# A one-core decoder layer in split float32: more loads on SyncE's queue, squares summed by ScalarE, and low parts of 22 weight pieces made by accumulating transfers

## The chip, the cores and the metric

The kernel runs on one core of a Trainium2 chip. The core has five engines with programs of their own: TensorE (PE, matmuls and transposes), VectorE (DVE), ScalarE (ACT), GpSimd (POOL) and SyncE (SP, here an issuer of transfers only). The metric is the device time of one launch in microseconds; the median of three runs is compared. The time before is 680.02 us (679.84 to 684.64).

## The reference, cut to what matters

One layer of a decoder trunk for 512 tokens of width 1024, all in float32:

```python
h = rmsnorm(x, norm_mix); mem_h = rmsnorm(mem, norm_mem)
proj = h @ w_in                                  # one input projection, cut into 8 parts
c_q, c_kv, k_rope, hq, hf, hi, hg, mq = split(proj)
y_mla = mla_group(c_q, c_kv, k_rope, ...)        # low-rank attention, causal, 4 heads
y_hg  = hgrn2_group(hq, hf, hi, hg, ...)         # gated linear recurrence, 4 heads
y_mem = mem_group(mq, mem_h, ...)                # cross-attention into 256 memory tokens
x = x + concat([rmsnorm(y_mla), y_hg, rmsnorm(y_mem)]) @ w_out
x = x + (silu(h2 @ w_gate) * (h2 @ w_up)) @ w_down      # h2 = rmsnorm(x), inner width 2816
```

`rmsnorm(x, g)` is `x * rsqrt(mean(x*x) + eps) * g`.

## The kernel before, in words

Activations are kept transposed, with features on the 128 partitions and the 512 tokens along the row; x is eight tiles of 128 x 512 (`xin`, tag "tm"). To keep float32 accuracy on PE, every operand is split into a high part, rounded to PE's float32r format, and a low part, the rest; `mm3` (L558) makes a product of three matmuls: high by high, high by low, low by high. `split` (L528) makes the parts: the high part is a cast on ACT, the low part a subtraction on DVE. The gain of the first norm is multiplied in while x is split; the factor 1/rms of each token is applied later, to products: `rx` (per token as a column) and `RX` (the same, spread over a 128 x 512 tile).

The program runs in this order. Twelve matmuls on constants come first (`WARM`, L437). Then x is loaded with the first columns of `w_in` (the `we` tiles, four feature blocks at once), split, and multiplied into four accumulators. `gated` makes the q and f parts of the recurrent group, `wide` (L735) its values, four 128-token blocks at a time, and `hg_levels` its decays. `lowrank` makes the compressed q and kv. The attention of the first group, the memory's keys and values, the cross-attention and the output projection follow, and from about 340 us on the FFN, in three column groups with seven products each for blocks of two by two (`seven`, L1410). There the sum of two weight blocks is already made by transfers which add to what lies in the destination: GpSimd issues them (`more`, L1424, `accum_op=ALU.add`).

Weights arrive by `load` (L536): 512 KB at a time into one of three 128 x 1024 tiles "wr", issued by SP. `piece` splits half a tile into a pair of 128 x 512 tiles, "wh" (five slots) and "wl" (four slots). In the FFN `part` also uses "wr" tiles for pairs.

Sums of squares: for x, ACT squares each of the eight tiles, DVE adds them up (`sumsq`), PE sums the result over the partitions with matmuls of 32 columns by 2 (`colsums`, `T.tiles`), and DVE makes the reciprocal root by some ten small steps (`rms`, `rsqrt_col`). For the memory the same is done with four tiles. 

What sets the order: nothing is issued while the program is recorded. `Recorder.record` lists every operation with its inputs and a priority (its number and a class, changed by the table `NUDGE`: from, to, shift), and `Recorder.run` then lays them out on five engines by estimated costs and free slots; some operations may be moved to another engine. `issue` emits them in that order, from L421 (PE's small tiles) and L424 (all the rest), so nearly all rows of the profile have one of these two lines, and the names of tiles tell them apart: "xh" and "xl" are the parts of x, "mx" and "v" the parts of the first weights, "at", "mm" and "tr" the accumulators' banks (three, three and two).

Of the kernel before, what the change touches and what calls it, by code (L numbers as in the profile page):

```python
# [47 lines left out]
class Recorder:  # L48
# [205 lines left out]
    def length(self, o):  # L254
# [3 lines left out]
        return 2 if o.name == "transpose" or o.kw["rhs"].dtype != F32 else 4  # L258


    IDLE = (1500, 3400)


    NUDGE = ((4523, 4572, -1208), (2899, 2922, 153), (3591, 3619, 261), (5080, 5112, 35), (5132, 5152, -187), (4881, 4888, -127), (833, 873, 7059), (4038, 4040, 343), (3730, 3774, 191), (4055, 4056, -1089), (5057, 5087, 605), (5096, 5097, 51), (5041, 5094, -195), (5387, 5394, 57), (3008, 3017, 415), (3705, 3738, -1018), (969, 989, -566), (5497, 5507, 388), (3048, 3063, 528), (4794, 4826, -14), (4034, 4058, 24), (5265, 5278, -2632), (5519, 5549, -317), (4066, 4083, -4), (968, 978, -1195), (4416, 4437, -227), (5057, 5066, -584), (3678, 3726, 79), (2213, 2230, 387), (3749, 3800, -698), (3952, 4008, -75), (290, 314, 354), (4141, 4157, 211), (586, 592, 790), (2631, 2650, 56), (3575, 3624, -28), (371, 421, 128), (5155, 5160, 312), (685, 697, 401), (2820, 2830, 265), (4487, 4528, -350), (763, 784, -147), (4472, 4519, 334), (1209, 1222, 357), (2030, 2049, -600), (3663, 3706, 33), (1550, 1566, 8), (369, 379, 609), (2292, 2334, 1893), (3104, 3108, -229), (3446, 3497, -146), (3458, 3487, 401), (5080, 5128, 17), (3070, 3075, 53), (2112, 2117, 110), (1594, 1603, -13), (1503, 1505, 92), (1400, 1404, 1034), (3047, 3065, -458), (2398, 2422, -345), (3844, 3904, -190), (3156, 3169, 94), (1128, 1180, -33), (3732, 3757, 144), (2990, 3037, -207), (3971, 3973, -124), (1839, 1844, -36), (1248, 1276, -13), (1792, 1793, -366), (158, 195, -424), (2647, 2648, 611), (5037, 5054, 66), (4876, 4882, -106), (1471, 1483, -459), (2041, 2058, -88), (2747, 2771, -122), (1486, 1489, 331), (1523, 1542, 1379), (693, 698, -494), (4462, 4511, -166), (1167, 1213, -456), (3349, 3388, 638), (1775, 1778, -455), (3988, 4008, -390), (1981, 2008, -332), (2573, 2761, -42), (1036, 1062, 17), (1336, 1355, 86), (675, 700, -238), (1554, 1556, -17), (1880, 1936, 59), (2818, 2836, -24), (3075, 3091, -674), (4376, 4379, 398), (731, 737, -425), (2690, 2706, -44), (2646, 2647, 42), (2917, 2971, -572), (4832, 4835, -140), (5153, 5162, 438), (4481, 4514, -137), (5422, 5428, 274), (3705, 3761, -89), (4234, 4235, -182), (1261, 1283, 34), (62, 109, -1000015), (1830, 1889, 12), (2099, 2105, 41), (3735, 3746, 267), (4336, 4337, 1074), (710, 740, -88), (2697, 2724, -320), (2183, 2208, -18), (2625, 2651, -21), (4345, 4401, -177), (4291, 4292, 38), (3298, 3301, -1000015), (2682, 2739, 63), (3480, 3487, -804), (629, 670, 295), (3160, 3163, -148), (506, 518, 651), (3695, 3706, -432), (59, 112, -15), (2898, 2925, 47), (5531, 5583, 85), (2275, 2320, -999980), (2355, 2360, -999779), (5131, 5139, 36), (2523, 2552, -11), (3090, 3546, -33), (1181, 1182, -4), (3436, 3446, 73), (3880, 3930, -29), (1824, 1825, -202), (543, 566, -23), (722, 758, 559), (1736, 1753, -372), (1890, 1897, -9), (2502, 2532, -5), (165, 167, 493), (5584, 5595, 398), (4277, 4283, 21), (4888, 4893, 37), (2286, 2317, 647), (3287, 3324, 419), (822, 884, -497), (2242, 2289, 81), (2797, 2822, -89), (1448, 1478, 373), (1100, 1164, 5), (2563, 2568, -8), (597, 604, 388), (3827, 3833, 55), (2186, 2188, 205), (558, 569, -25), (817, 860, 405), (2749, 2796, -79), (3691, 3740, -109), (2604, 2716, 54), (4296, 4345, -525), (3222, 3238, -12), (5421, 5451, 334), (2642, 2653, 4), (2042, 2047, 655), (4097, 4148, 5), (2643, 2666, -47), (4973, 4974, 614), (4924, 4927, 36), (552, 567, 653), (3734, 3738, -105), (726, 727, -195), (4433, 4436, 151), (4710, 4711, 303), (5121, 5134, -12), (4502, 4550, -60), (503, 512, -603), (3731, 3736, 544), (3839, 3851, -13), (1180, 1184, 101), (3659, 3694, 52), (5258, 5622, -1035), (5522, 5533, 84), (2598, 2602, 41), (2394, 2411, 45), (849, 857, -233), (2961, 2977, 85), (2625, 2657, -152), (139, 181, -39), (1176, 1182, 305), (3429, 3430, -555), (4813, 4828, 6), (893, 946, 81), (4741, 4745, 17), (3304, 3348, -251), (1057, 1079, -612), (4202, 4231, -64), (374, 405, 161), (5386, 5625, 1000335), (2718, 2754, -1000022), (2645, 2647, 4), (3911, 3957, 21), (3971, 4017, 33), (2755, 2781, 564), (5202, 5217, -999393), (2812, 2821, 17), (5518, 5557, -114), (2442, 2452, -175), (4376, 4419, 25), (4811, 4835, 8), (2472, 2500, -52), (1746, 1788, 413), (4968, 4969, 508), (1150, 1211, 451), (4566, 4588, -192), (1898, 1916, -5), (1400, 1411, 417), (3557, 3654, -8), (2519, 2521, 130), (2693, 2698, 180), (3237, 3290, 11), (3775, 3779, 268), (2140, 2143, 57), (4141, 4153, 14), (2237, 2240, 187), (3139, 3141, 177), (677, 684, 54), (1788, 1791, -237), (3385, 3418, 24), (2394, 2412, 54), (2524, 2550, -13), (1887, 1901, 19), (3423, 3485, -72), (4991, 5053, 35), (3834, 3844, -59), (1153, 1164, -8), (3326, 3345, 218), (3302, 3317, -567), (1923, 1972, 828), (4940, 4941, 63), (4555, 4581, 224), (2297, 2359, -29), (4778, 4807, -998879), (1766, 1771, -78), (2837, 2854, 7), (252, 266, 415), (246, 279, -363), (3968, 3972, -612), (5235, 5249, -10), (1534, 1544, -588), (3486, 3502, -1000043), (5217, 5226, -357), (5611, 5625, -72), (4595, 4615, -184), (4896, 4916, 266), (1756, 1791, 11), (3224, 3227, -171), (4428, 4443, -6), (2740, 2757, 171), (513, 519, -1000400), (1665, 1716, 690), (5093, 5096, -296), (3135, 3182, 17), (1773, 1789, 51), (656, 673, -363), (5199, 5203, -53), (5201, 5257, 328), (4968, 5016, -50), (1569, 1575, 376))

    def run(self):
        ops = self.ops
        for a, b, d in self.NUDGE:
            for o in ops[a:b]:
                o.prio += d  # L270
# [21 lines left out]
        while done < len(ops):  # L292
# [89 lines left out]
            for k in o.new:  # L382
                tag = self.tiles[k][0]
                slots[tag].remove(min(slots[tag]))
                order[tag].remove(k)
# [1292 lines left out]
```

## Time and profile before

| | |
|---|---|
| median of 3 runs | 680.02 us |
| profiled execution | 681.25 us |
| its span, first to last instruction | 679.5 us |
| PE busy | 672.0 us |
| DVE busy | 590.7 us |
| ACT busy | 396.1 us |
| POOL busy | 100.1 us |
| bytes moved | 95.16 MB |

The span is what the rows below divide; the profiled execution is 1.75 us longer than it. PE's busy time counts a matmul until its results have passed, so neighbouring matmuls overlap in it (a row of 0.39 us every 0.23 us), and how fast PE works is read from the starts. An accumulating transfer has its own queue in the list of queues (software_dynamic), since GpSimd issues it; SP's and ACT's are hardware_dynamic.

### The profile page before, as it was taken

The page shows a single profiled execution, that of the slowest core. Times are in us where ns is not written, and L with a number is a line of the kernel's source. Part 1 is how long each engine was busy: PE and PEld are TensorE (multiplying, and loading weights), DVE is VectorE, ACT ScalarE, POOL GpSimd, SP SyncE. Part 2 cuts the span into 40 slices and gives each one's busy share as a digit, 9 for nine tenths or more (in the row PEclk, how much of TensorE's full clock was granted, in tenths as well). Part 3 has the DMA queues.
Part 4 walks back from the last instruction along what each step waited for, and adds up shares of the span by engine and source line. Part 5 has one row for each costly group of instructions (what it writes and reads, how often), then busy time and mean ns, then how long its engine had stood idle before and what let it go on. Part 6 is the DMA issues. An engine that isn't in the chain of part 4 may idle for free.

```text
span 679.5 us, 12872 instructions
## 1 busy us (share of the span) xinstructions
PE 672.0 (99%) x4686; PEld 563.7 (83%) x4686; DVE 590.7 (87%) x1316; ACT 396.1 (58%) x779; POOL 100.1 (15%) x134
## 2 busy tenths in 40 slices
PE   9999999999999999999999999999999999999997
PEld 5889987788887888788888888888888899889986
DVE  6878889769989889887989989779898979998996
ACT  7674355547667665765577555456545554754662
POOL 1000000000000000000023222323222223323320
PEclk9999999999999999999999999999999999999999
DMA  9512320014233243134358887987977789978755
GB/s 314 169 50 68 123 75 29 32 65 139 79 125 125 77 140 110 31 110 156 109 128 155 219 197 186 172 204 172 207 166 171 160 176 215 202 163 178 161 101 143
DMA packets 48159, 95.16 MB, mean 140 GB/s; under 512 B 5472, under 2 KB 13536, under 8 KB 48096
## 3 DMA queue, kind: packets, MB, share of 16 engines
q1 hardware_dynamic: 32256, 67.33, 30.3%
q0 software_dynamic: 15120, 25.96, 24.1%
q10 hardware_dynamic: 720, 1.05, 0.5%
q8 instruction: 37, 0.61, 0.4%
q14 instruction: 26, 0.21, 0.1%
HBM read 92.22 MB, written 2.10 MB: 139 GB/s over the span
## 4 chain that ended last, share of the span: by engine, by line
PE 94%; DVE 3%; DMA 1%; ACT 1%; issue 0%; SPq 0%; DVEq 0%
PE mm L424 54%; PE at L424 32%; PE tr L424 6%; PE at L421 1%; DMA tm<-in_xT 1%; DVE sm L424 1%; PE tr L421 1%; DMA tm<-in_xn 1%; DVE y L424 0%; DVE tc L424 0%; DVE tm L424 0%; DVE hd L424 0%; DVE wl L424 0%; DVE v L424 0%; SPq L424 0%
## 5 line engine op out<-in xcount | busy, mean ns | idle before, releaser
L424 ACT CAST wr<-mx 128x512 fp32r<-128x512 f32 (+1 forms) x78 | 45.7, 595 | 40.0 <-PE at L424 25.7
L424 ACT CAST wh<-wr 128x512 fp32r<-128x512 f32 (+2 forms) x75 | 43.9, 597 | 40.7 <-PE mm L424 28.8
L424 DVE TENSOR_TENSOR wr<-mx,wr 128x512 fp32r<-128x512 f32 (+1 forms) x94 | 60.6, 655 | 6.3 <-ACT wr L424 5.0
L424 DVE TENSOR_TENSOR wl<-wr,wh 128x512 fp32r<-128x512 f32 (+2 forms) x84 | 54.9, 657 | 8.3 <-PE mm L424 6.7
L424 ACT CAST wh<-mx 128x512 fp32r<-128x512 f32 (+1 forms) x74 | 43.8, 598 | 30.3 <-PE at L424 16.2
L424 PE MATMUL mm<-xh,wh 128*128 128x512 f32 x136 | 53.8, 396 | 0.4 <-DVE hd L424 0.4
L424 PE MATMUL mm<-xl,wh 128*128 128x512 f32 x136 | 54.1, 399 | 0.0
L424 DVE TENSOR_TENSOR wl<-mx,wh 128x512 fp32r<-128x512 f32 (+1 forms) x81 | 51.9, 654 | 2.5 <-PE at L424 2.0
L424 PE MATMUL mm<-xh,wl 128*128 128x512 f32 x136 | 53.4, 394 | 0.0
L424 POOL DMA_DIRECT2D mx<-in_wg x36 | 31.6, 950 | 121.5 <-DVE wr L424 78.6
L424 PE MATMUL mm<-wh,xh 128*128 128x512 f32 (+2 forms) x136 | 47.2, 371 | 0.0
L424 ACT CAST wh<-y 128x512 fp32r<-128x512 f32 (+1 forms) x51 | 30.1, 594 | 28.2 <-PE at L424 13.7
L424 PE MATMUL mm<-wh,hd 128*128 128x512 f32 (+2 forms) x140 | 44.7, 366 | 0.3 <-DVE qr L424 0.3
L424 PE MATMUL mm<-wh,mx 128*128 128x512 f32 x128 | 43.6, 401 | 0.0
L424 POOL DMA_DIRECT2D mx<-in_wu x36 | 31.4, 936 | 81.9 <-DVE wr L424 31.9
L424 POOL DMA_DIRECT2D mx<-in_wd x33 | 28.8, 938 | 71.8 <-DVE wl L424 50.5
L424 DVE TENSOR_TENSOR wl<-y,wh 128x512 fp32r<-128x512 f32 (+1 forms) x52 | 33.2, 649 | 2.1 <-PE at L424 1.2
L424 POOL MEMSET pb<- 128x128 f32 x15 | 2.8, 205 | 214.8 <-PE at L424 203.6
L424 PE MATMUL mm<-wl,xh 128*128 128x512 f32 (+2 forms) x92 | 32.8, 359 | 0.0
L424 PE MATMUL mm<-v,xh 128*128 128x512 f32 x96 | 31.8, 401 | 0.0
L424 PE MATMUL at<-wh,xh 128*128 128x512 f32 x88 | 31.5, 391 | 0.0
L424 PEld LDWEIGHTS mm<-xh,wh 128*128 128x128 f32 x136 | 25.6, 188 | 5.8 <-DVE hd L424 0.9
(469 smaller groups left out, 1950.0 us busy)
## 6 DMA issues: line engine op xcount, KB each, us to landing
wr<-in_wf SPq DMA_DIRECT2D x17, 512.0 KB, 3.7
mx<-in_wd POOLq DMA_DIRECT2D x33, 256.0 KB, 4.6
wr<-in_wo SPq DMA_DIRECT2D x12, 512.0 KB, 3.7
mx<-in_wg POOLq DMA_DIRECT2D x24, 256.0 KB, 6.1
mx<-in_wu POOLq DMA_DIRECT2D x24, 256.0 KB, 5.8
mx<-in_wd SPq DMA_DIRECT2D x22, 256.0 KB, 4.0
y<-in_wd SPq DMA_DIRECT2D x22, 256.0 KB, 4.5
wr<-in_wt SPq DMA_DIRECT2D x8, 512.0 KB, 3.2
```

Of the source, the lines that this page charges most:

```text
L421: r = self.nc.tensor.matmul(get(a), lhsT=get(b), rhs=get(c), start=first, stop=last, skip_group_check=True)
L424: r = getattr(getattr(self.nc, o.eng), o.name)(*[get(a) for a in o.args], **{k: get(a) for k, a in o.kw.items()})
```

## The change: what it does

- The weights of x's first tiles are issued by SP for all tiles but the first (before, ACT issued those of the first four), and the number of warm-up matmuls is 9 instead of 12.
- `squares` replaces the sums of squares of x and of memory: x (and memory) is loaded once more with tokens on the partitions, ACT squares each half row and sums it in the same instruction (`accum_out`), and one DVE addition joins the halves. The additions of `sumsq` and the column sums on PE are left out for these two.
- `load` is gone. Each piece of 512 columns or fewer is its own transfer of up to 256 KB into one of six 128 x 512 "wr" tiles.
- For 22 pieces (features 0 to 4, `wva` and `wvb`, named in `MADE`) the low part is made in another way: ACT writes minus the high part into "wl", and a transfer issued by GpSimd adds the weight itself to it.
- In `softmax` the small negation moves from DVE to ACT.
- The planner is told a shorter landing time for early transfers, and `NUDGE` has 249 other entries instead of 269.

```diff
-    NUDGE = ((4523, 4572, -1208), (2899, 2922, 153), (3591, 3619, 261), ...
+    NUDGE = ((2674, 2759, 2137852), (4855, 4871, -117), (3907, 3920, 369), ...
...
-WARM = 12
+WARM = 9
 FIRST = 4
-EARLY = {k: (1, ("wr", "p", "p", "tc", "tc", "tc", "hd", "hd")[k]) for k in range(8)}
-XLAG = 0
+EARLY = {k: (1, ("qr", "p", "p", "tc", "tc", "tc", "hd", "hd")[k]) for k in range(8)}
+MADE = {0: 'S', 1: 'S', 2: 'S', 3: 'S', 4: 'S', 'wva': 'S', 'wvb': 'S'}
...
-        "wr": 3, "wh": 5, "wl": 4, "xh": 8, ...
+        "wr": 6, "wh": 5, "wl": 4, "xh": 8, ...
...
+    def piece(src, a, b, made=False, tags=("wh", "wl")):
+
+        w = slice(0, b - a)
...
+        raw = sb("wr")[:, w]
+        hi = sb(tags[0], dt=F32R)[:, w]
+        lo = sb(tags[1], dt=F32R)[:, w]
         with rec.first(0):
-            split(raw[:, a:b], hi[:, :b - a], lo[:, :b - a])
+            DMA.dma_start(out=raw, in_=src[:, a:b])
+            if made:
+                A.copy(hi, raw)
+                A.activation(lo, f(hi), AF.Copy, scale=-1.0)
+                G.dma_start(out=lo, in_=src[:, a:b], accum_op=ALU.add)
+            else:
+                split(raw, hi, lo)
         return hi, lo
...
-                    (A if k < 4 else DMA).dma_start(out=w, in_=t["we"][k - 1])
+                    DMA.dma_start(out=w, in_=t["we"][k - 1])
...
-    xs = None
-    for k in range(KD):
-        with rec.after(xdone[min(KD - 1, k + XLAG)]), rec.first(0):
-            xs = sumsq(xraw[k:k + 1], xs, "td", V)
...
+    def squares(src, nb, tag, cls):
+
+        v = small(2 * nb).rearrange("p (b j) -> p b j", j=2)
+        for b in range(nb):
+            for j in range(2):
+                r = sb(tag)
+                with rec.first(cls):
+                    DMA.dma_start(out=r, in_=src[b, j])
+                A.activation(sb("td"), r, AF.Square, accum_out=v[:, b, j:j + 1])
+        r = small(nb)
+        V.tensor_tensor(r, v[:, :, 0], v[:, :, 1], ALU.add)
+        V.tensor_scalar(r, r, RC / D, RC * EPS, ALU.mult, ALU.add)
+        return rsqrt_col(r, nb)
...
-        V.tensor_copy(rx, rms(xs, D))
+        V.tensor_copy(rx, squares(t["xn"], NB, "y", -1))
...
-            ms = sumsq([r.rearrange("p a b -> p (a b)")], ms)
-        ms2 = sb("td", (P, NM))
-        V.tensor_tensor(ms2, ms[:, :NM], ms[:, NM:], ALU.add)
         rm = cp.tile([P, 2], F32, name="rm")
-        vm = small(2)
-        V.tensor_scalar(vm, colsum(ms2, 2), RC / D, RC * EPS, ALU.mult, ALU.add)
-        V.tensor_copy(rm, rsqrt_col(vm, 2))
+        V.tensor_copy(rm, squares(t["mem"], 2, "y", 1))
...
-        V.tensor_scalar(m, m, neg, None, ALU.mult)
+        A.activation(m, m, AF.Copy, scale=neg)
```

How the order moves is shown at three places, with the line of the kernel, the operation, its output and inputs, and its size.

PE at the start, from the last warm-up matmul on ("tr" from a constant), before:

```order
L424 MATMUL tr_1797<-const-bfloat16-1.0 128x512
L424 MATMUL at_1860<-xh_1851,mx_1843 128x512
L424 MATMUL mm_1863<-xh_1851,mx_1843 128x512
L424 MATMUL at_1869<-xh_1851,mx_1843 128x512
L424 MATMUL at_1860<-xl_1858,mx_1843 128x512
L424 MATMUL at_1860<-xh_1851,v_1846 128x512
```

and in the changed kernel:

```order
L426 MATMUL tr_1962<-const-bfloat16-1.0 128x512
L426 MATMUL at_2009<-xh_2000,mx_1992 128x512
L426 MATMUL at_2009<-xl_2007,mx_1992 128x512
L426 MATMUL at_2009<-xh_2000,v_1995 128x512
L426 MATMUL at_2023<-xh_2000,mx_1992 128x512
L426 MATMUL at_2025<-xh_2000,mx_1992 128x512
```

The low part of x ("xl") is asked for by the second matmul now, by the fourth before.

GpSimd's program behind its first memsets, before (the memsets after "tm" belong to the attention):

```order
L424 MEMSET tm_1975 128x512
L424 MEMSET tm_1996 128x512
L424 MEMSET pb_3477 128x128
L424 MEMSET pb_3481 128x128
L424 MEMSET pb_3538 128x128
```

and in the changed kernel, where ten more accumulating transfers from in_wf stand behind the twelve from in_wva and in_wvb:

```order
L426 MEMSET tm_2134 128x512
L426 MEMSET tm_2144 128x512
L426 DMA wl_2425<-in_wva 128x320
L426 DMA wl_2477<-in_wva 128x320
L426 DMA wl_2501<-in_wva 128x320
L426 DMA wl_2523<-in_wva 128x320
L426 DMA wl_2563<-in_wva 128x320
```

The 22 transfers have one fixed order on GpSimd's queue, ahead of the memsets of the attention.

PE in the changed kernel where the values of the recurrent group begin ("mm_2520", "mm_2528", "tr_2537" and "tr_2544" are the accumulators of four token blocks, "wh" and "wl" the weight's parts). First the end of the group ahead and the first piece:

```order
L426 MATMUL mm_2468<-xl_2171,wh_2356 128x512
L426 MATMUL mm_2468<-xh_2166,wl_2398 128x512
L426 MATMUL mm_2520<-wh_2391,xh_2000 128x320
L426 MATMUL mm_2520<-wl_2425,xh_2000 128x320
L426 MATMUL mm_2520<-wh_2391,xl_2007 128x320
```

and, 36 rows further, the first matmul with the low part of the fourth piece:

```order
L426 MATMUL mm_2528<-wl_2501,xh_2062 128x320
L426 MATMUL mm_2528<-wh_2466,xl_2072 128x320
L426 MATMUL mm_2528<-wh_2498,xh_2088 128x320
L426 MATMUL mm_2520<-wl_2523,xh_2088 128x320
L426 MATMUL mm_2520<-wh_2498,xl_2097 128x320
L423 MATMUL at_2623<-pth_2318,tm_2482 32x32 x16
```

Between the last use of wl_2398 and the first of wl_2523 stand 40 matmuls of 320 columns.

## Rows read from the trace of the kernel before

**Rows 1.** The page's first part: busy time, share of the span and instructions of each engine.

```profile
PE 672.0 (99%) x4686; PEld 563.7 (83%) x4686; DVE 590.7 (87%) x1316; ACT 396.1 (58%) x779; POOL 100.1 (15%) x134
```

**Rows 2.** The page's slices, 40 of 17 us each: PE's granted clock in tenths, and GB/s of the transfers.

```profile
PEclk9999999999999999999999999999999999999999
...
GB/s 314 169 50 68 123 75 29 32 65 139 79 125 125 77 140 110 31 110 156 109 128 155 219 197 186 172 204 172 207 166 171 160 176 215 202 163 178 161 101 143
```

**Rows 3.** The timeline of PE in the FFN, from 440 us on: start, length in us, engine, line, operation, output and inputs.

```profile
439.94 0.39 PE L424 MATMUL mm<-wr,hd 128*128 128x512 f32 x1
440.17 0.39 PE L424 MATMUL at<-wh,hd 128*128 128x512 f32 x1
```

**Rows 4.** The page's chain of work that ended last, by engine.

```profile
PE 94%; DVE 3%; DMA 1%; ACT 1%; issue 0%; SPq 0%; DVEq 0%
```

**Rows 5.** The list of what PE waited for: tile and engine waited for, us in total, times, longest.

```profile
PE tr L421 <- issue: 0.9, 1, 0.9
PE tr L424 <- PEq L1667: 0.8, 1, 0.8
PE at L424 <- ACT xh L424: 0.6, 1, 0.6
PE mm L424 <- DVE hd L424: 0.4, 1, 0.4
PE mm L424 <- DVE qr L424: 0.3, 1, 0.3
PE at L424 <- ACT mx L424: 0.3, 1, 0.3
PE mm L424 <- DVE xl L424: 0.2, 1, 0.2
```

**Rows 6.** The timeline at the start (PE, ACT and DVE) and, in the last line, PE's last matmul. In brackets the idle time before and what ended it.

```profile
0.78 4.95 PE L424 MATMUL tr<-const-bfloat16-1.0 128*128 128x512 bf16 x12 [0.78 <-PEq L1667]
...
5.55 0.72 ACT L424 ACTIVATE xh<-tm,wr 128x512 fp32r<-128x512 f32 x1 [2.40 <-DMA wr<-in_web]
...
6.31 0.75 DVE L424 SCALAR_TENSOR_TENSOR xl<-tm,wr,xh 128x512 fp32r<-128x512 f32 x1 [1.94 <-ACT xh L424]
...
6.33 0.50 PE L424 MATMUL at<-xh,mx 128*128 128x512 f32 x1 [0.60 <-ACT xh L424]
...
6.73 0.50 PE L424 MATMUL mm<-xh,mx 128*128 128x512 f32 x1
...
7.07 0.39 PE L424 MATMUL at<-xh,mx 128*128 128x512 f32 x1
...
9.80 0.50 PE L424 MATMUL at<-xh,mx 128*128 128x512 f32 x1 [0.26 <-ACT mx L424]
...
675.24 0.39 PE L424 MATMUL mm<-wh,xh 128*128 128x512 f32 x1
```

**Rows 7.** Starts on PE around the column sum of x (the matmul ahead of it and the second one behind it, a line that merges two), and pieces of the chain of waits in order of time (start, us, what): the column sum of memory, and the matmuls behind the column sums in which PE waited longest.

```profile
21.65 0.39 PE L424 MATMUL at<-xh,mx 128*128 128x512 f32 x1
...
22.67 0.62 PE L424 MATMUL at<-xh,v 128*128 128x512 f32 x2
...
95.04 0.24 PE tr L421 x16
...
136.46 2.49 PE mm L424 x10
```

**Rows 8.** Groups of instructions with shapes kept apart: busy us, mean ns of one, and idle time before them.

```profile
L424 DVE TENSOR_TENSOR wl<-wr,wh 128x512 fp32r<-128x512 f32 x73 | 49.7, 685 | 4.6 <-PE mm L424 3.7 <-issue 0.4
L424 DVE TENSOR_TENSOR wl<-wr,wh 128x320 fp32r<-128x320 f32 x8 | 3.9, 489 | 2.4 <-PE mm L424 1.7 <-ACT ptl L424 0.5
L424 DVE TENSOR_TENSOR td<-td,td 128x512 f32<-128x512 f32 x12 | 8.2, 683 | 0.0
L424 ACT CAST wh<-wr 128x320 fp32r<-128x320 f32 x7 | 3.2, 457 | 8.9 <-PE mm L424 8.9
```

**Rows 9.** The timeline of DVE behind the column sum of x: the first and the last small step of the root (ten of them, with others between).

```profile
22.80 0.15 DVE L424 TENSOR_SCALAR sd<-tr 128x4 f32<-128x4 f32 x1
...
25.72 0.16 DVE L424 TENSOR_TENSOR rx<-rx 128x4 f32<-128x4 f32 x1
```

**Rows 10.** Busy time by stretches: from and to, its length, busy us of PE, PEld, DVE, ACT and POOL with counts, PE's granted clock, DMA share, GB/s.

```profile
50.00:100.00 50.00, 50.00 (x1098) 45.27 (x1099) 43.99 (x130) 22.60 (x48) 0.00 (x0) 1.00 0.25 84
...
100.00:160.00 60.00, 58.30 (x658) 48.69 (x646) 49.03 (x141) 33.31 (x75) 1.56 (x8) 1.00 0.19 67
336.00:680.00 344.00, 339.62 (x1625) 289.26 (x1623) 303.17 (x538) 190.20 (x351) 90.82 (x104) 1.00 0.78 172
```

**Rows 11.** Accumulating transfers of the FFN: the page's median from issue to landing for one group, the transfers issued at 411.47 and at 659.53 us by themselves, and from the page's groups POOL's time for issuing one (mean ns).

```profile
mx<-in_wd POOLq DMA_DIRECT2D x33, 256.0 KB, 4.6
...
mx<-in_wu POOLq DMA_DIRECT2D x1, 256.0 KB, 7.2
...
mx<-in_wd POOLq DMA_DIRECT2D x1, 256.0 KB, 3.8
...
L424 POOL DMA_DIRECT2D mx<-in_wu x36 | 31.4, 936 | 81.9 <-DVE wr L424 31.9
```

**Rows 12.** Pieces of the chain of waits in order of time: matmuls of 320 columns, and one group of small tiles.

```profile
52.12 3.66 PE tr L424 x25
55.78 1.23 PE at L421 x82
```

More of the change, by code (lines that the diff above doesn't have):

```diff
@@ L381, in run @@
                 end = dma + (3400 if o.eng == "gpsimd" else 2500)
+                if o.eng != "gpsimd" and t < 1400:
+                    end -= 1400 - t
             for k in o.new:
@@ L733, in chunk, with wide @@
         return src[a * P:b * P].rearrange("(p c) -> p c", p=P)
[L735 to L737 removed]
+    def wide(src, n, banks, acts, use, made=False):
+        per = S // n
         with rec.first(2):
             for j in range(0, KD, per):
[L740 to L744 removed]
+                p = piece(chunk(src, j * n, (j + per) * n), 0, per * n, made)
+                for k in range(j, j + per):
+                    w = cut(p, slice(None), slice((k - j) * n, (k - j + 1) * n))
                     for b, o in enumerate(banks):
@@ L1024, in sq_heads @@
         V.tensor_reduce(dst, s_, AX.X, ALU.add)
-    wuq = [load(t["wuq"][k], 768) for k in range(3)]
     qr = sb("qr", (P, NB, 4, 64))
@@ L1030, in body @@
     qf = []
-    w = [piece(r, 0, 512) for r in wuq]
+    w = [piece(t["wuq"][k], 0, 512, MADE.get("wuq")) for k in range(3)]
     sq = []
@@ L1043, in body @@
     V.tensor_copy(sq_n.rearrange("p b h -> p h b"), colsums(sq))
-    w = [piece(r, 512, 768) for r in wuq]
+    w = [piece(t["wuq"][k], 512, 768, MADE.get("wuq")) for k in range(3)]
     for b in range(NB):
@@ L1088, in body @@
     rope(kr.unsqueeze(2), 1)
-    wukv = [load(t["wukv"][k]) for k in range(2)]
     kn = [None] * NB
@@ L1095, in body @@
     for i in range(2):
-        w = [piece(r, i * S, (i + 1) * S) for r in wukv]
+        w = [piece(t["wukv"][k], i * S, (i + 1) * S, MADE.get("wukv")) for k in range(2)]
         for b in range(NB):
@@ L1287, in wout @@
         r = []
-        for a in range(0, len(ks), 2):
-            raw = sb("wr", (P, 1024))
-            with rec.first(0):
-                DMA.dma_start(out=raw, in_=t["wo"][j, ks[a] // 2])
-            for i in range(2):
-                v = (sb("wh", dt=F32R), sb("wl", dt=F32R)) if len(r) < keep else (sb("v", dt=F32R), sb("v", dt=F32R))
-                with rec.first(0):
-                    split(raw[:, i * S:(i + 1) * S], *v)
-                r.append(v)
+        for k in ks:
+            r.append(piece(t["wo"][j, k], 0, S, MADE.get("wo"), ("wh", "wl") if len(r) < keep else ("v", "v")))
         return r
```

81 lines of the change are left out of this document (31 added, 50 removed).

## The prediction

> **What bounds the kernel now.** I read the busy totals first [rows 1]: TensorE (PE) is busy for 672.0 of 679.5 us, VectorE (DVE) for 590.7, ScalarE (ACT) for 396.1, GpSimd (POOL) for 100.1. The slices [rows 2] show a granted clock of nine tenths or more throughout, the higher of its two levels (2.4 GHz). Since a busy PE may still be slow, I then looked at starts of neighbouring matmuls late in the run [rows 3]: 0.23 us apart for 512 columns, some 2.25 columns per ns, with nothing left between them. The chain that ended last is 94% PE [rows 4]. The list of PE's waits [rows 5] sums to 3.5 us: 0.8 before the first instruction, 0.6 before the first real matmul, and 2.1 in five waits after that. The timeline [rows 6] gives the ends: first real matmul at 6.33, last one at 675.24.
>
> So this is a kernel with PE as its bound almost everywhere. What the change saves on DVE is worth only the PE waits that DVE causes. The most that can be won is PE's own removed work, 2.1 us of waits and perhaps a little of the 6 us before the first matmul.
>
> **Base.** The profiled execution took 681.25 us (span 679.5 and 1.75 around it). The median of the runs is 680.02, 1.23 below it. I form differences in the profiled execution and apply them to 680.02.
>
> **Part by part.**
>
> *Squares.* The eight-fold DVE sums of x's squares and their column sum on PE go. Its cost on PE: from the start at 21.65 to the one at 22.67 lie two matmuls and the column sum, 1.02 us [rows 7]; two matmuls at 0.23 are 0.46, so 0.56 us. The memory's column sum is half as long and stands with 0.24 us in the chain [rows 7]. Both are PE time on the path: -0.8 us in all. On DVE eleven additions of 0.68 go [rows 8], 7.5 us, beside PE work. In exchange x is loaded a second time in natural layout, 2.1 MB, and memory again, 1.0 MB. The transfers of x and of the first weights (4.5 MB) and the new 2.1 MB at the 314 GB/s of the first slice [rows 2] are done by 21 us; ACT, which starts at 5.55 and has sixteen operations of at most 0.72 first [rows 6], has squared the last of them by about 22. In the kernel before, the small DVE steps of the root took from 22.80 to 25.72 [rows 9], so rx is there at about 25. PE asks for it in the new order after 107 matmuls, 6.33 + 0.7 (a wait, below) + 107 x 0.23 = 31.6 us. Six microseconds of cover: cost 0. The next weight piece, behind x on SyncE's queue, lands at 22, is split by 23.5 and is asked for after 89 matmuls, at 27.5: cost 0. The narrowest place is the evacuation behind RX: with half a microsecond each for transposes and copy RX is there near 33, DVE then has three products, a subtraction and a cast of at most 0.68 each [rows 8] until 36.4, and the fourth accumulation in the mm banks asks at 36.5 (nineteen matmuls behind the transposes). If this slips, it slips by a few tenths.
>
> *Three warm-up matmuls fewer.* They lie before 6.33, and PE idled 0.6 there, so their removal wins nothing: the first matmul waits for ACT, ACT for the transfer of in_web [rows 6]. The idle gap grows from 0.6 to about 1.8 us. The twelve ran at the lower clock level (4.95 us, 0.41 each, 512 columns at 1.24 per ns [rows 6]); the first real ones start 0.40 and then 0.34 us apart, so the level had risen by 6.73. Bounds: if it rises when it did, 0; if it takes the same 5.95 us from 6.33 on, at half speed, +3.0. I take the value between, where PE must make up the missing 1.2 us of slow work: half of it lost, +0.6.
>
> *Weights of the first tiles issued by SyncE.* ACT loses three issues. The second matmul now needs xl, which DVE ended at 7.06, so PE idles 0.7 us there; eleven more at 0.23 end near 9.8, and it was 9.80 when PE before got on after a wait for a weight [rows 6]. That weight came from ACT's third transfer; as SyncE's second it lands earlier, and this wait of 0.3 us goes. Net 0.
>
> *Accumulating transfers.* 22 subtractions (eight of 0.49, fourteen of 0.68 us [rows 8]) leave DVE, 13 us; as many negated copies come, four of the eight narrow ones on DVE. DVE is busy for 88% from 50 to 100 us and 82% from 100 to 160, ACT for 45% and 56% [rows 10], so both have room. POOL, idle for most of that stretch, gets 22 issues of 0.94 us [rows 11]. What counts is time to landing: from free slot to first use a low part now needs a release of 0.2, a copy of 0.46 at most [rows 8], and the transfer. Accumulating transfers of 256 KB took 3.8 us at the least and 7.2 at the most, 4.6 in the median of one group, in a stretch where DMA is 78% busy [rows 10, 11]. Here DMA is 25% busy, so I take the low end, 3.8 to 4.6: need 4.5 to 5.3 us. The tightest piece is wl_2523: the tile four before it, wl_2398, whose slot it takes, is last read just ahead of the first 320-column matmul, and wl_2523 is asked for 40 such matmuls later, 40 x 0.146 = 5.9 us [rows 12]. The next piece has 36 of them and a 1.23 us group of small tiles, 6.5 us. Cost 0, with little to spare; by the largest landing the need is 7.9 us and the tightest piece is 2.0 late.
>
> The Trainium skill, "DMA: Bandwidth & Descriptors", section "SWDGE vs HWDGE vs iDMA", speaks against this part: GpSimd writes descriptors into rings in on-chip memory, and DVE's two-port modes lock it out. In this trace an issue took 0.94 us in the mean with DVE 88% busy [rows 10, 11], and no row shows one held. By the row the sum stays; by the rule, as an estimate with two DVE operations of 0.49 us ahead of each issue, the need grows to 5.5 to 6.3 us and the tightest piece is up to 0.4 late: 679.2 instead of 678.8, and rival 1 is likelier.
>
> *Order.* The whole table of numbers is new, so PE's five waits after the start need not recur. The longest, 0.9 us, comes inside six column sums that stood almost in a row [rows 5]; in the new order they stand in groups of two and four, some eight microseconds of PE work apart. The three waits for DVE fall in the stretch where DVE is relieved or shortly after. I take half of the 2.1 us as gone, -1.1; bounds: all gone (-2.1), or as much again on top (+2.1). Splitting 512 KB loads into two leaves the bytes alone; 25 small negations on ACT lengthen no PE wait that I can name. FFN: same operations, same slots, PE dense; 0.
>
> **Sum.** -0.8 + 0.6 + 0 - 1.1 = -1.3: a profiled execution of about 680.0 and a median of **678.8 us**.
>
> **Rivals.**
> 1. *Late low parts* (slower). Each wide piece waits for its transfer if landing takes over 5.2 us after issue. For: 7.2 occurs, and POOL's order is fixed, so one late copy delays the next. Against: the quiet DMA here. A delay shifts all later windows, so only the slot's own turns add up; 2.0 for wl_2523, 1.1 for the piece behind it in its slot (38 matmuls and a small-tile group, 6.8 us), then nothing: 3.1 us. Time 680.0 - 0.8 + 0.6 + 3.1 = 682.9, with no wait saved. Chance 0.2.
> 2. *Clock at the lower level at the start*: 3.0 instead of 0.6, so 681.2. For: the gap trebles; against: the 0.9 us of idling inside the column sums [rows 5] changed no distance behind it (ten matmuls in 2.49 us [rows 7]). Chance 0.12.
> 3. *All waits go and nothing new comes*: 680.0 - 0.8 - 2.1 = 677.1, and up to 1 us more from the earlier first weights: 676. Chance 0.2.
> 4. *A new order with longer waits elsewhere*, a chain of several engines that no single row shows, 5 us or more: 685 and above. The old order holds at 2.1 us of waits over 670, so such a thing would be new. Chance 0.08.
> Forecast proper: 0.4.
>
> **How the numbers follow.** Rivals 3 and 1 with their tails set the range: 675.0 to 684.5. About 1%, 6.8 us, is what a measurement of this kernel can surely tell from no change. Faster by more would need under 673.2, below PE's own work: 0.03. Slower by more needs over 686.8, rivals 1, 2 and 4 together or 4 alone: 0.06. Within: 0.91.
>
> **What would show it.** Right: the page with PE near 670 us busy and a similar chain; DVE 20 to 30 us lower and ACT 10 to 20 higher; no column sum before 50 us; 22 POOL issues between 45 and 115 us landing in 3.8 to 4.6 us; no PE wait on a DMA. Wrong on the low parts: PE waits that end with "DMA wl<-in_wva". Wrong on the clock: starts 0.43 us apart after the first matmul, or a granted clock below the top in the first 20 us. Wrong on the order: the sum of PE's waits after 10 us above 4 us. The whole forecast falls if the distance between 512-column matmuls in the dense stretches changes from 0.23 us: 0.01 us there is some 20 us.

## The result, and the profile after

The changed kernel took 678.02 us (median of 17 runs, 676.80 to 680.90), the kernel before, run beside it, 681.12 us (17 runs, 679.84 to 685.14): a ratio of 0.9948 with a 95% interval of 0.993 to 0.9966, or 3.5 us less (2.3 to 4.8). By my bound of 1% this is no change; as a difference of half a per cent it is clear, for the interval leaves out 1. The profiled execution took 677.61 us with a span of 675.6, against a span of 679.5.

One thing must be known to read the times below: "at full clock" means the median of those runs of a kernel whose mean granted clock was 0.999 or more, which is 680.28 us for the kernel before (62 of the 77 runs taken beside the experiments; the other 15 have 682.76) and 677.61 after (13 of 17), so -2.7 us.

The page of the changed kernel, its busy totals, granted clock and chain by engine, which answer to [rows 1, 2, 4]:

```profile
PE 667.6 (99%) x4635; PEld 564.2 (84%) x4635; DVE 561.0 (83%) x1259; ACT 420.5 (62%) x843; POOL 118.9 (18%) x155
...
PEclk9999999999999999999999999999999999999999
...
PE 96%; DVE 2%; issue 0%; ACT 0%; DMA 0%; ACTq 0%
```

PE is still the bound and has 4.4 us less to do; DVE lost 29.7 us, ACT gained 24.4, POOL 18.8. The timeline at the start, as in [rows 6], with the transfers that ACT issues (ACTq):

```profile
0.74 0.41 ACTq L426 DMA_DIRECT2D qr<-in_wea  x1
...
1.18 0.45 ACTq L426 DMA_DIRECT2D qr<-in_web  x1
...
4.04 0.72 ACT L426 ACTIVATE xh<-tm,qr 128x512 fp32r<-128x512 f32 x1 [0.88 <-DMA qr<-in_wea]
...
4.82 0.50 PE L426 MATMUL at<-xh,mx 128*128 128x512 f32 x1 [0.63 <-ACT xh L426]
...
5.60 0.50 PE L426 MATMUL at<-xl,mx 128*128 128x512 f32 x1 [0.28 <-DVE xl L426]
...
5.94 0.39 PE L426 MATMUL at<-xh,v 128*128 128x512 f32 x1
```

The first real matmul starts at 4.82 instead of 6.33, and the last at 671.19 instead of 675.24. Of the 4.05 us between the ends 1.51 lie ahead of the first matmul and 2.54 behind it. PE's waits, as in [rows 5]:

```profile
PE tr L426 <- issue: 0.8, 1, 0.8
PE tr L426 <- PEq L1663: 0.8, 1, 0.8
PE at L426 <- ACT xh L426: 0.6, 1, 0.6
PE tr L426 <- DVE qr L426: 0.5, 1, 0.5
PE mm L426 <- DVE v L426: 0.4, 1, 0.4
PE tr L426 <- ACT tm L426: 0.4, 1, 0.4
PE at L426 <- DVE xl L426: 0.3, 1, 0.3
```

They sum to 3.8 us, no less than before. In place of the wait of 0.9 us put on "issue" one of 0.8 stands elsewhere, and none ends with a transfer. Busy time by stretches, as in [rows 10], and the 22 accumulating transfers between 40 and 130 us (count, KB each, median us from issue to landing), as in [rows 11]:

```profile
50.00:100.00 50.00, 48.76 (x1023) 44.37 (x1022) 36.91 (x121) 27.64 (x61) 14.90 (x17) 1.00 0.83 170
100.00:160.00 60.00, 59.89 (x701) 50.38 (x700) 50.71 (x150) 37.30 (x82) 3.29 (x10) 1.00 0.26 73
```

```profile
wl<-in_wf POOLq DMA_DIRECT2D x10, 256.0 KB, 5.0
wl<-in_wva POOLq DMA_DIRECT2D x8, 160.0 KB, 4.5
wl<-in_wvb POOLq DMA_DIRECT2D x4, 256.0 KB, 6.8
```

Between 50 and 100 us the DMA engines are now 83% busy instead of 25%, and DVE has 7.1 us less to do.

### The profile page after: what moved, and what is told of

It is laid out like the page before. It is cut to its first block, busy times and chain, and to the rows that moved or that the text cites. A ratio compares the mean times of both kernels' runs of the same rounds, so it can differ in the third digit from the quotient of the medians.

```text
span 675.6 us, 13020 instructions
## 1 busy us (share of the span) xinstructions
PE 667.6 (99%) x4635; PEld 564.2 (84%) x4635; DVE 561.0 (83%) x1259; ACT 420.5 (62%) x843; POOL 118.9 (18%) x155
## 4 chain that ended last, share of the span: by engine, by line
PE 96%; DVE 2%; issue 0%; ACT 0%; DMA 0%; ACTq 0%
PE mm L426 55%; PE at L426 33%; PE tr L426 6%; PE at L423 1%; PE tr L423 1%; DMA qr<-in_wea 0%; DVE wl L426 0%; DVE hd L426 0%; DVE td L426 0%; DVE qr L426 0%; DVE tm L426 0%; ACT wh L426 0%; DVE y L426 0%; DVE xl L426 0%; DVE sq_r L426 0%
## 5 line engine op out<-in xcount | busy, mean ns | idle before, releaser
L426 ACT CAST wh<-wr 128x512 fp32r<-128x512 f32 (+2 forms) x67 | 40.0, 604 | 22.1 <-PE mm L426 17.3
L426 DVE TENSOR_TENSOR wl<-wr,wh 128x512 fp32r<-128x512 f32 (+1 forms) x62 | 41.0, 673 | 5.5 <-ACT wh L426 4.1
L426 ACT CAST wh<-y 128x512 fp32r<-128x512 f32 (+1 forms) x48 | 28.2, 592 | 21.6 <-PE at L426 11.0
L426 PEld LDWEIGHTS mm<-xh,wl 128*128 128x128 f32 x136 | 25.6, 188 | 5.1
L426 PEld LDWEIGHTS mm<-xl,wh 128*128 128x128 f32 x136 | 25.6, 188 | 4.9
```

What stands on the lines that cost most here:

```text
L426: r = getattr(getattr(self.nc, o.eng), o.name)(*[get(a) for a in o.args], **{k: get(a) for k, a in o.kw.items()})
```

## The experiments

Nearly all edits below change the finished list of operations (`order`, just behind `rec.run()`), so that the planner's order stays as it is and only the named thing moves. Where two kernels have the same order on PE, I laid the starts of their matmuls side by side; "shift" is that difference at a time.

### Why the first matmul comes earlier

In the kernel before ACT's own program, read from its list of instructions (in brackets the counter of finished transfers that it waits for), begins so:

```
1 L424 DMA wr_1800<-in_wea 128x136
2 L424 DMA wr_1800<-in_web 128x384
3 L424 ACT_TABLE_LOAD
4 L424 ACTIVATE hpi<-ones 128x1 [waits DVE_49]
5 L424 DMA p_1818<-in_we 128x512
6 L424 DMA p_1823<-in_we 128x512 [waits DMAHW0_49]
7 L424 DMA tc_1828<-in_we 128x512 [waits DMAHW2_49]
8 L424 ACTIVATE xh_1851<-tm_1804,wr_1800 128x512 [waits DMAHW1_49]
```

In this program SP's and ACT's transfers take eight counters (DMAHW0 to 7) in turn, and the ninth is made to wait until the first, which has the same counter, has landed. Counter 0 is in_wea, 1 x's first tile, 2 in_web. So instruction 7 waits for in_web, and xh, which needs only counters 0 and 1, stands behind it. The trace of the kernel before has these two issues on ACT, ahead of xh at 5.55 in [rows 6]:

```profile
3.81 0.34 ACTq L424 DMA_DIRECT2D p<-in_we  x1
5.17 0.34 ACTq L424 DMA_DIRECT2D tc<-in_we  x1
```

**SP issues them in the kernel before** (b_sp_issue):

```diff
+    for o in order:
+        if o.dma and o.eng == "scalar" and o.kw["in_"].tensor.name == "in_we":
+            o.eng = "sync"
```

> The kernel before with one thing changed: the three transfers of the first weights that ACT issued are issued by SP, at the same places of the written order; all else, operations and order, is left. Theory 1 (in the kernel before ACT's program is held at an issue: the fifth transfer that it issues waits until the 192 KB of in_web have landed, at 5.17, and takes 0.34 us, and only then comes the operation xh of the first x tile, at 5.55; nothing that xh itself needs was so late): xh begins near 4.1, the first real matmul near 4.9 instead of 6.33, and the time falls by 1.0 to 1.5 us, a ratio of 0.998. Theory 2 (the prediction's: xh waits for data, and what SP's queue takes over costs as much as it gives): the first matmul stays between 6.0 and 6.5, the time within 0.3 us. Theory 3 (the shorter start is what made nearly all of the 3.5 us): the ratio is 0.995.

```profile
3.92 0.72 ACT L424 ACTIVATE xh<-tm,wr 128x512 fp32r<-128x512 f32 x1 [0.76 <-DMA wr<-in_wea]
...
4.96 0.58 PE L424 MATMUL at<-xh,mx 128*128 128x512 f32 x1
```

In this timeline xh starts at 3.92, the first matmul at 4.96. The shift is -1.40 us from 25 us on and stays between -1.33 and -1.40 until 135; nothing takes it back. There another 1.1 comes (the wait of 0.9 us on "issue" does not occur in this execution; more on it below), and the last matmul is 2.4 earlier. Ratio 0.9989 (0.9971 to 1.0007), at full clock 679.12, 1.2 less than before. The interval of the ratio takes in "no change"; the trace and the runs at full clock show the gain. Theory 1.

**ACT issues them, one later in its program** (b_act_late: the third is put behind the high part of in_web):

```diff
+    moved = [o for o in order if o.dma and o.eng == "scalar" and o.kw["in_"].tensor.name == "in_we"][2:]
+    order = [o for o in order if o not in moved]
+    at = [n for n, o in enumerate(order) if o.eng == "scalar" and o.name == "copy" and o.args[0].tensor.name.startswith("mx")][0] + 1
+    order[at:at] = moved
```

> The kernel before with one issue moved within ACT's own program: ACT still issues all three, but the last of them (the one that waited for in_web) stands behind xh and behind the high part of in_web. Theory 1 (place in ACT's program): xh near 4.15, one issue of 0.34 us behind in_wea's landing at 3.81, first matmul near 4.95, as with all three on SP, time -1.0 to -1.4 us. Theory 2 (which queue carries the bytes, or data that xh needs): first matmul unchanged, 6.0 to 6.5, time within 0.3 us.

```profile
3.91 0.33 ACTq L424 DMA_DIRECT2D p<-in_we  x1
...
4.30 0.72 ACT L424 ACTIVATE xh<-tm,wr 128x512 fp32r<-128x512 f32 x1 [1.14 <-DMA wr<-in_wea]
...
5.07 0.54 PE L424 MATMUL at<-xh,mx 128*128 128x512 f32 x1
...
5.26 0.35 ACTq L424 DMA_DIRECT2D tc<-in_we  x1
```

The queue is the same as before, only the place differs, and the first matmul starts at 5.07: the place in ACT's program decides. Shift -1.2 at 30 us, -1.8 at the end. The time shows less: ratio 1.0001 (0.998 to 1.0023), at full clock 679.51, 0.8 less; the times alone would not tell this kernel from the one before.

**The fault put back** into the changed kernel (a_act_wait, which also let the small score tiles wait for one tile more and so got another order; then a_act_wait2, with this edit alone):

```diff
+    at = [n for n, o in enumerate(order) if o.name == "activation" and o.args[0].tensor.name.startswith("xh")][0]
+    moved = [o for o in order[at:] if o.dma and o.eng == "sync"][:3]
+    moved[2].eng = "scalar"
+    order = [o for o in order if o not in moved]
+    order[at:at] = moved
```

> The changed kernel with the fault put back by another transfer: the issue of the x tile number 4 goes from SP to ACT, ahead of xh; it must wait for the landing of the weights of tile 1 (near 5.5). Theory 1: xh begins at 5.5 to 5.9 instead of 4.04, first matmul at 6.3 to 6.7 instead of 4.82, time +1.5 to +1.9 us against the changed kernel, a ratio of 0.997 to 0.998 to the kernel before. Theory 2: an issue on ACT costs its 0.4 us alone, first matmul by 5.3, ratio 0.995 to 0.996.

The first try had its first matmul at 6.18 and a ratio of 1.006 (1.0038 to 1.0082), but with another order, so only its start counts.

> The changed kernel with one thing changed: the issue of x tile 4 goes from SP to ACT, ahead of xh, where it waits for the landing of the weights of tile 1. (The first try of this also let the small score tiles wait for one tile more, which gave another order of the whole program; that is taken out, every other operation and its order is that of the changed kernel.) Theory 1 (place in ACT's program): first matmul 1.36 us later than in the changed kernel, as in the first try, and that shift is carried to the end: +1.2 to +1.8 us, ratio 0.9965 to 0.9975 to the kernel before. Rival (a later start upsets waits further on, as the first try's 682.0 us of span seems to say): +4 us or more, ratio above 1.0.

```profile
4.82 0.34 ACTq L426 DMA_DIRECT2D tm<-in_xT  x1
...
5.26 0.72 ACT L426 ACTIVATE xh<-tm,qr 128x512 fp32r<-128x512 f32 x1 [2.10 <-DMA p<-in_we]
...
6.03 0.49 PE L426 MATMUL at<-xh,mx 128*128 128x512 f32 x1 [1.25 <-ACT xh L426]
```

One issue that has to wait, ahead of xh, and most of the early start is gone: shift +1.2 until 40 us, +1.3 at 70, +2.1 from 75 on (the wait on "issue" near 77 us is 1.6 instead of 0.8), +0.8 at the end. Ratio 0.9984 (0.9969 to 1.0), that is 2.4 us above the changed kernel's. The start is Theory 1's; at the end I had expected +1.2 to +1.8, and trace and time lie on either side of that. Part of any delay is taken back late: from 589 to 632 us all five kernels made from the changed one with its order kept, whatever their shift, gain 1.1 us on it, and at 632 the changed kernel itself waits 0.5 us for DVE. The rival's +4 us falls: it stood only in the first try, with its other order.

### The accumulating transfers

**Replaced by DVE additions** (a_dve_low):

```diff
+        if o.dma and o.eng == "gpsimd" and o.kw["out"].tensor.name.startswith("wl"):
+            hi = next(p for p in rec.ops if p.n == o.n - 2)
+            o.eng, o.name, o.dma = "vector", "tensor_tensor", False
+            o.args, o.kw = (o.kw["out"], hi.args[1], f(o.kw["out"]), ALU.add), {}
```

> The changed kernel with the 22 accumulating transfers replaced, each at its place in the order, by an addition on DVE of the weight (already in the raw tile) to the negated high part. Output the same. DVE gets 22 operations of 0.49 to 0.68 us, 13 us, POOL loses 22 issues, 4.7 MB fewer are moved. Theory 1 (the prediction: these parts lie beside PE's work on either engine, price 0): ratio 0.994 to 0.996, as the changed kernel. Theory 2 (relief of DVE is part of the gain): +1 to +2 us, ratio 0.997 to 0.998, with new PE waits for DVE between 50 and 110 us. Theory 3 (the transfers are late or hold DVE or POOL back): faster than the changed kernel by 0.5 us or more, ratio 0.993 or below.

Ratio 0.9955 (0.9939 to 0.9971), at full clock 677.89 against 677.61. PE's waits:

```profile
PE mm L426 <- DVE v L426: 1.0, 1, 1.0
...
PE at L423 <- DVE tm L426: 0.7, 2, 0.4
PE at L423 <- DVE y L426: 0.6, 1, 0.6
```

Theory 2 has its waits (2.3 us, shift +1.7 at 110), but by the end of the span 0.7 is left, and 0.3 in the time. By these numbers the relief of DVE is worth between 0 and 0.7 us.

**Issued later** (a_late):

```diff
+        if o.dma and o.eng == "gpsimd" and o.kw["in_"].tensor.name == "in_wva":
+            again.append(o.n - 1)
+    order = [x for o in order for x in [o] * (4 if o.n in again else 1)]
```

> The changed kernel with the negated copy of each of the eight narrow pieces (in_wva) written four times instead of once (same values): their transfers are issued about 1.0 to 1.4 us later. In the changed kernel the tightest of them is issued at 50.64 and its low part is asked for at 55.37, 4.73 us later, and the transfers took 3.5, 4.5 and 5.3 us (least, median, most). Theory 1 (the low parts are just in time): PE waits appear between 50 and 66 us, 1 to 3 us in sum, and the end moves by 0.5 to 3 us, ratio 0.9955 to 0.999. Theory 2 (there is room enough): no new wait, ratio 0.994 to 0.996.

```profile
PE tr L426 <- DMA wl<-in_wva: 1.9, 2, 1.3
PE mm L426 <- DMA wl<-in_wva: 1.3, 3, 0.7
```

The first issue came at 42.96 instead of 41.21, the fourth at 53.47 instead of 50.64. Five waits for in_wva appear, the shift is +5.2 at 70 us and +3.6 at the end; ratio 1.0015 (1.0003 to 1.0026), 4.6 us above the changed kernel (4.0 at full clock). Theory 1, and dearer than I had put it. The five waits are 3.2 us; that the copies also kept ACT and DVE, and that one late piece delayed the next, is my reading of the rest and not tested.

### The warm-up and the clock

**Nine instead of twelve, alone** (b_warm9):

```diff
+    warm = [o for o in order if o.name == "matmul" and o.kw["rhs"].dtype == BF16]
+    order = [o for o in order if o not in warm[9:]]
```

> The kernel before with 9 warm-up matmuls instead of 12, all else left. The prediction's term: the first real matmul stays at 6.3, the idle time before it grows from 0.6 to 1.8 us, and half of the missing slow work has to be made up at the lower clock level: +0.6 us. Theory 1 (the level rises with the time that PE has been at work, idle or not in between): 0, starts 0.40, 0.34, then 0.23 us apart as before. Theory 2 (the missing work has to be done in full): +1.2 to +3.0 us, the first six or more real matmuls 0.4 us apart.

```profile
7.12 0.49 PE L424 MATMUL at<-xh,mx 128*128 128x512 f32 x1 [2.34 <-ACT xh L424]
7.52 0.50 PE L424 MATMUL mm<-xh,mx 128*128 128x512 f32 x1
7.86 0.43 PE L424 MATMUL at<-xh,mx 128*128 128x512 f32 x1
8.09 0.62 PE L424 MATMUL at<-xl,mx 128*128 128x512 f32 x1
8.51 0.63 PE L424 MATMUL at<-xh,v 128*128 128x512 f32 x1
```

in_web landed 0.8 later in this execution (near 5.96, by chance as far as I can tell), and xh, held behind it, with it. PE stood idle for 2.34 us, began at the upper level (granted clock 1.00 until 8 us), and then the matmuls from 8.09 to 11.50 us came 0.43 apart (granted clock 0.50 from 9 to 11). Shift +1.8 at 10 us: 0.8 from the later start, 1.0 from the clock. A second drop (0.60 from 138 to 142) makes it 2.9. Ratio 1.0046 (1.0028 to 1.0064), 3.1 us; at full clock (2 of 10 runs) 681.84, 1.6 more than before. Theory 2, in that matmuls had to be done at the lower level; but here the idle time was 2.34 us and not the 1.8 that the term had, so the term itself is not priced by this.

**Twelve with the early start** (a_warm12), three more warm-up matmuls in the changed kernel:

> The changed kernel with 12 warm-up matmuls again, a look at the start alone. Theory (with the earlier start the three are in the way): the warm-up ends near 5.6 to 5.9, the first real matmul starts there instead of at 4.82, and 20 us into the span PE is 0.3 to 0.6 us later than in the changed kernel. Rival: the level rises earlier with three more, and nothing is lost.

The first real matmul starts at 5.47 instead of 4.82, but then xl is ready: the second follows at 5.88, the third at 6.12 (5.60 and 5.94 in the changed kernel). Shift +0.16 at 20 us and -0.03 at the end (one execution). Of the rival, the part that nothing is lost.

**None at all** (a_warm0):

```diff
+    order = [o for o in order if not (o.name == "matmul" and o.kw["rhs"].dtype == BF16)]
```

> The changed kernel with no warm-up matmuls at all. Theory 1 (the first real matmuls have to do the warm-up's work at the lower level): first matmul at 4.8 as before, then some 10 to 14 matmuls 0.41 us apart instead of 0.23: +1.8 to +2.6 us at 10 us into the span, and the same at the end. Rival (what is lost at the start is made good while PE waits for x anyway): less than +0.7 us at the end.

The first matmul starts at 4.79, those from 6.17 to 9.15 stand 0.43 apart, shift +1.8 at 10 us and +1.5 at the end; ratio 0.9974 (0.9957 to 0.999), 1.8 us above the changed kernel (1.5 at full clock). Theory 1.

### The column sums, and the order

**Left out, with SP issuing** (b_sp_nosum): b_sp_issue, and

```diff
+    sums = [o for o in order if o.name == "tiles" and o.args[1].tensor.name.startswith("ones")]
+    for o in [sums[0]] + [o for o in sums if Recorder._free(o.args[2]) == NM]:
+        o.eng, o.name, o.args, o.kw = "vector", "memset", (o.args[0], 512.0), {}
```

> The kernel before with SP issuing the first weights, as in the first experiment, and without the column sums of x's and memory's squares on PE: DVE fills their places with a constant, so the two norm factors are not computed here (the additions on DVE stay). It is the kernel before with the two parts of the change that I now hold for its gain, and with neither the new order nor the accumulating transfers. Theory 1 (start -1.4, column sums -0.8): the first matmul near 4.9, a step of -0.5 to -0.6 us more at 22 us and of -0.25 near 95 us, ratio 0.9955 to 0.998. Rival (the new order or the low parts carry a good part): ratio 0.998 to 1.0, as with SP alone (0.9989).

I expected a gain of 0.8 on top and got none: ratio 1.0013 (1.0001 to 1.0026), at full clock 679.96 (4 of 12 runs), 0.8 more than b_sp_issue. The shift against the kernel before goes from -1.17 at 20 us to -1.76 behind the place of x's column sum, where b_sp_issue stays at -1.40: the column sum of x is worth 0.6 at its place. It goes back to -1.32 at 25, where four transposes read rx:

```profile
24.24 0.17 DVE L424 COPY rx<-sd 128x4 f32<-128x4 f32 x1
...
24.48 0.41 PEld L424 LDWEIGHTS tr<-cst,rx 128*128 128x128 f32 x4 [0.64 <-issue]
```

The profile puts this wait on "issue", but the first weight load starts 0.07 us after DVE has written rx (24.41), as it does in the kernel before (25.75 after 25.68). PE, being earlier, now waits for rx; in the changed kernel no wait stands there. The column sum of memory gives 0.1 at 95 us. Between 130 and 140 us all is lost: +0.65, where b_sp_issue has -2.45. Busy time by stretches there (PE's granted clock is the third column from the end):

```profile
130.00:134.00 4.00, 3.57 (x157) 2.52 (x155) 3.49 (x14) 1.78 (x3) 0.39 (x2) 1.00 0.39 126
134.00:138.00 4.00, 3.05 (x53) 2.58 (x54) 1.80 (x12) 0.95 (x2) 0.00 (x0) 0.82 0.02 4
138.00:142.00 4.00, 4.00 (x22) 3.37 (x21) 1.76 (x3) 0.26 (x2) 0.00 (x0) 0.76 0.00 0
```

PE waits 1.37 us on "issue" among the six column sums that stand there, and behind this the clock is below full: 0.18 and 0.24 of 4 us are 1.7 us, with the wait 3.1, which is nearly the whole loss (-2.51 to +0.65).

**The column sum of x nine times** (b_col9):

```diff
+    col = [o for o in order if o.name == "tiles" and o.args[0].tensor.name.startswith("tr")][0]
+    at = order.index(col)
+    order[at:at] = [col] * 8
```

> The kernel before with the column sum of x's squares issued nine times in a row instead of once (same result), to price one: by the prediction's term 0.56 us each, +4.5 us at 22 us into the span; if 0.56 is in good part the change from 512-column matmuls to small ones and back, then as the neighbouring column sums stand to each other in the trace, 0.28 us each, +2.2 us. A floor on both by instruction fetching would show as idle time among them.

```profile
21.92 1.40 PE L421 MATMUL tr<-ones,td 128*32 128x2 f32 x147
24.88 1.23 PE L421 MATMUL tr<-ones,td 128*32 128x2 f32 x128 [1.56 <-issue]
28.61 0.38 PE L421 MATMUL tr<-ones,td 128*32 128x2 f32 x13 [2.50 <-issue]
```

Neither number: +8.7 us at 25 us into the span and +11 in the time (ratio 1.0161, 1.0138 to 1.0183). The narrow matmuls themselves take little, 32 of them 0.31 us (a quarter of 1.23); over 4 us are two waits on "issue" ahead of one block of 128 and of the next, and behind the first the granted clock is 0.58 and 0.57 from 26 to 34 us. A second drop of the clock near 146 us adds 1.6.

**The table of numbers emptied** (a_plain, `NUDGE` without effect in the changed kernel):

> The changed kernel with an empty NUDGE table: every operation keeps its own priority, and the planner lays out another order. It prices what the table of numbers is worth, the size of the prediction's term on the order and of its rival 4. If the planner's rules alone already keep PE busy: within 1.5 us of the changed kernel. If the table carries waits of several engines: +5 us or more, ratio above 1.002, with PE waits between 50 and 340 us.

```profile
PE mm L423 <- issue: 2.4, 1, 2.4
PE mm L423 <- DVE hd L423: 2.0, 1, 2.0
PE mm L423 <- DVE xh L423: 1.7, 1, 1.7
```

Ratio 1.0104 (1.009 to 1.0119): the table is worth 10.6 us in the changed kernel (1.0104 less 0.9948; 8.3 by the one run at full clock). The waits lie not only between 50 and 340 us as I expected, but at 361, 378 and 665 too.

## Why the prediction was right, and where not

678.8 was forecast and 678.02 measured, inside the range and within 1%; by ratio the gain is 3.5 us, at full clock 2.7, where I forecast 1.3, and three terms of the sum were off. That the number came so near is in part luck: my base, 680.02, was the median of three runs, 1.1 below that of the seventeen.

*Weights of the first tiles issued by SyncE* is the step that failed: a wait that I took for fixed. I priced it "Net 0" and wrote that "the first matmul waits for ACT, ACT for the transfer of in_web", reading the releaser in [rows 6] as something that xh needs. xh reads x's first tile and the gain in in_wea; what waited for in_web was the issue in front of it. It measured -1.4 us in the trace (b_sp_issue) and -1.2 at full clock, it is undone by one waiting issue (a_act_wait2), and it follows the place in ACT's program and not the queue (b_act_late). It is the largest single piece of the gain that an experiment shows.

*Three warm-up matmuls fewer* was put at +0.6 with the idle gap growing to 1.8 us. In the changed kernel the gap is 0.63, since the first matmul came earlier, and starts are 0.23 apart from 5.94 on: 0, and twelve would do as well (a_warm12). The reasoning itself holds for the edit alone: with a late start and 2.34 us of idle time b_warm9 lost about 1.0 us to the clock there. One reading in it was wrong: starts 0.40 and then 0.34 us apart are no sign of the clock, for b_warm9 has the same two at a granted clock of 1.00. Two edits that I had priced apart depend on each other.

*Squares* at -0.8 was nearly right at the places (0.6 and 0.1 for my 0.56 and 0.24) and did not add up in the old order: in b_sp_nosum a wait for rx, 0.4 us, and a wait on "issue" with the clock behind it, some 3 us near 135, took more back than was won. I had taken PE's time as a sum of its matmuls; among narrow ones PE can also wait for instructions, and where it does depends on how many came before.

*Order* at -1.1, half of the waits gone, did not come so: the waits behind the first matmul are 2.4 us where they were 2.1. What is left of the gain at full clock is 2.7 - 1.2 = 1.5 us for *Squares* and *Order* together, which I had put at 1.9. The runs don't divide it: taking the sums out of the old order gives nothing, and emptying the table costs 10.6. The two profiles say where it shows. Counted from each start to the next, without waits, the matmuls of two columns take 0.78 us less than before, those of 512 columns, 2173 in both kernels, 2.65 less, and all other float32 ones 0.61 more; and the lead is all won ahead of the FFN's last 1500 matmuls, where it is 4.3 us, against 4.05 at the end. So the new order gains in the pace of PE and not in its waits; why the wide matmuls stand closer in it stays open.

*Accumulating transfers* at 0 was right (0 to 0.7 us gained), and so was the warning on the tightest piece. wl_2523 was issued at 50.64 and asked for at 55.37:

```profile
50.64 0.86 POOL L426 DMA_DIRECT2D wl<-in_wva  x1 [1.44 <-DVE wl L426]
...
55.37 0.31 PE L426 MATMUL mm<-wl,xh 128*128 128x320 f32 x1
```

These are 4.73 us; it took 4.23 and landed 0.5 us ahead of its use. The transfers of that size took 3.5, 4.5 and 5.3 us (least, median, most) with the DMA at 83%, not at the quiet 25% that I counted on. The landing times that I took, 3.8 to 4.6, were short for the larger pieces (5.0 and 6.8), which had 6.6 us at the least between issue and first use; the one with the least landed 0.3 us ahead. So the price of 0 held by a few tenths, with landing times that I had wrong. Rival 1's 3.1 us for pieces two microseconds late was of the right kind: a_late cost 4.6. On the rule of the Trainium skill that I weighed ("DMA: Bandwidth & Descriptors", "SWDGE vs HWDGE vs iDMA"): no issue by POOL took over 1.11 us, with DVE 74% busy, so no row shows one held here either, and the sum without the rule was the right one.

Rival 2 (the clock) did not happen in the changed kernel, but does in b_warm9. Rival 3 (677.1) is nearest to the result, with another cause than the one I gave it: the waits did not go, the first matmul came earlier. Of my signs, ACT's rise (24.4 us, not 10 to 20) and those landing times were outside. My aside in rival 3 of "up to 1 us more from the earlier first weights" was the effect that mattered.

## What to carry to other kernels

A transfer's issue is an instruction of the engine that makes it: if it must wait, everything behind it in that engine's program waits too (xh starts at 5.26 instead of 4.04 us in a_act_wait2), and the profile then names the transfer as the releaser of an operation which does not read it. Before pricing a wait, compare the releaser with the operands; the same holds for "issue", which in b_sp_nosum stands at a wait for rx. And edits that meet at one place (an earlier start, a shorter warm-up) are to be priced together.

## What I had not expected of the hardware

PE's waits of 0.4 us or more on "issue" stand at fixed places in its count of instructions. From the start of the span to just before such a wait, PE and PEld have these counts (b_col9, its first three waits; in brackets after PE's and PEld's busy time):

```profile
0.00:24.87 24.87, 21.89 (x223) 14.81 (x223) 17.39 (x32) 17.53 (x31) 2.39 (x9) 1.00 0.74 256
0.00:28.60 28.60, 23.12 (x351) 15.95 (x351) 17.39 (x32) 17.53 (x31) 2.39 (x9) 0.97 0.67 233
0.00:144.34 144.34, 137.40 (x1880) 114.22 (x1881) 112.08 (x309) 77.31 (x152) 3.96 (x17) 0.98 0.31 101
```

446, 702 and 3761 instructions: from the first to the second exactly 256, to the third 13 x 256 less 13. The kernel before waits after 3249, the changed one after 1465, b_sp_nosum near 135 us after 3248, a_plain after 1213 and 1722; divided by 256 all leave 176 to 190. Counted by the records that start before PE falls idle, the fourteen such waits, in eleven kernels, all leave the same, 193. And the traces have the transfers: in each of the fourteen one of 16 KB on the instruction queue had started 2.2 to 2.6 us before PE went on, in b_col9 at 22.50, 26.18 and 141.96. In the middle of its second wait, from 26.0 to 27.4 us, it is the only transfer there is (packets, MB, share):

```profile
q8 instruction: 1, 0.02, 4.9%
```

So instructions arrive in blocks of 256, and PE waits where it has used up one before the next is there. In b_col9 the next came 3.7 us after the last (24.88 to 28.61), while 128 narrow matmuls with their weight loads took 1.23; a 512-column matmul every 0.23 us uses a block in some 30 us. The Trainium skill, "Runtime: NRT & Kernel Launch", "Instruction fetch mechanics", has the blocks of 256 and calls the crossing mostly hidden; the traces agree: each kernel fetches 36 to 39 blocks of 16 KB and waits for none to three of them, always behind runs of matmuls of 256 columns or fewer. So taking narrow matmuls out, as the change does, also moves every later block against the places where narrow ones stand close together, for better or worse: at the six column sums near 135 us the same order on PE waited 0.9 us in the kernel before, 0.6 in b_warm9 and not at all in b_sp_issue, where the block's transfer started 6.5 us ahead of the place, and in the kernel before 1.5. Why executions differ there no run tells.

Behind such waits the clock can fall: 0.82 and 0.76 after 1.37 us (b_sp_nosum), 0.58 and 0.57 after 1.56 and 2.50 (b_col9), 0.60 after 0.65 (b_warm9), and not after the 0.94 of the kernel before, the 1.60 of a_act_wait2 or the 2.36 of a_plain. All these drops stand behind column sums, but the kernel before waits there too. So the length of the wait alone does not decide it, and what does no run tells.
